# SSM outputs spilled in four parts and reloaded into slots of their own, softmax reciprocals spread by a TensorE product, and two buffers for the SSM input operator

## The chip, the core and the metric

The kernel runs on one core of a Trainium2 chip. A core has five engines that each work through an instruction list of their own, strictly in its order: PE (TensorE, matrix products), DVE (VectorE), ACT (ScalarE), POOL (GpSimd) and SP (SyncE, which here only issues DMAs). They wait for each other through semaphores. The metric is the device time of one execution in microseconds (us); less is better.

## What is computed

One layer of an encoder on 512 tokens of width 1024, cut here to its stages:

```
h = x + 1/2 * SwiGLU_1(RMSNorm(x))                      # FFN 1, width 2816
u = RMSNorm(h);  q, k, v, x_ssm, g_attn, g_ssm = split(u @ W_in)
y_attn = attention(rope(norm(q)), rope(norm(k)), v) @ W_attn_branch   # 8 heads of 64, 2 k/v heads
y_s5   = S5_forward(x_ssm) + S5_backward(x_ssm) + D * x_ssm           # 32 groups x 16 channels
z      = gelu(y_s5);  z = z * sigmoid(z @ W_glu + b_glu)
y_ssm  = z @ W_ssm_branch
h = h + (sigmoid(g_attn) * y_attn + sigmoid(g_ssm) * y_ssm) @ W_out
h = h + 1/2 * SwiGLU_2(RMSNorm(h))                      # FFN 2
out = h + sigmoid(RMSNorm(h) @ W_ple_gate) * (p @ W_ple_proj)
```

The softmax of a head is computed as exp(s - max), multiplied with v, and only then divided by the row sums. The reciprocals of these sums lie with one token per partition, and the products they scale have one channel per partition and the tokens along the free dimension, so the reciprocals have to be turned round and repeated over 64 partitions.

## The kernel before

Each float32 product is made of three products of a high and a low part (`mm3`, lines 559 to 561), with 512 columns of output in one PSUM bank. A weight chunk is loaded by SP (`wchunk`, L554), split into its two parts by ACT (L544) and DVE (L545), and then used by PE. There are four raw buffers and four of each part. Tile names in the trace end in letters such as `w_617h` for the high part of weight chunk 617.

The part that the change touches is the mixer, from 440 to 730 us of the trace:

1. **Projections.** x_ssm (tile `X`) goes to DRAM (`xs_d`) and comes back in another layout as `U`, which ACT and DVE split into three bf16 parts (L33 to L36). k, v (`pk`) and q (`pq`) follow.
2. **SSM blocks.** 16 blocks (`ssm_block`) of two groups each. In a block PE multiplies `U` with the input operator `wv` into `pv` (24 small products, L43). DVE then runs nine operations: a rotation (L463 to L465), two scans (L473, L474), the rotation back (L477 to L479). PE adds the direct part (`ml`, L43) and the output operator (`wol`, L485) into `py`, and ACT writes the gelu into tile `Z`. The operators of a block are prefetched by SP: `wv` has one buffer, the table `tbl`, `wol` and `ml` two each. Between the blocks stand products of the twelve first gates (`gate`, bank `pi`, 24 products each), and DVE also does q's rotary embedding and normalisation.
3. **Attention.** For each head `scores` makes four products pairs `sc`, DVE a negated maximum (`nb`), ACT the exponentials `p` with their sums (`s2`). `values` transposes `p` on PE (`ppt`, 4 x 128x128), ACT and DVE split the result into `ph` and `pl`, PE multiplies with v into `po`. At the end of a head ACT copies half of `po` to `ob` and DVE adds the other half into `of`. After each second head `of` is multiplied with `R`, the reciprocals spread over partitions, and split into `oT`. `fill` gives PE other work beside the heads: four more gates, then the GLU of z (`w_521`, `w_554` are its weight chunks), then the SSM branch.

After the last block `Z` goes to DRAM in 8 DMAs (`zs_d`). `z_load` brings it back with channels on partitions as four tiles `zT`, which ACT and DVE split into `z`. The four `zT` lie in slots of the normalised input (`x4l` to `x7l`), which the gates' products read. The reciprocals go to DRAM as `r_d`, one 4-byte number after the other, and come back as `R` by a DMA that repeats each row over 64 partitions. All of these DMAs are in SP's list, between the weight loads.

A scheduler sets the order of the instructions on each engine from the program, with priorities; a tile's slot is handed on when its last reader is done.

Of the kernel before, what the change touches and what calls it, by code (L numbers as in the profile page):

```python
# [17 lines left out]
P = 128  # L18
SEQ = 512
# [408 lines left out]
def ssm_prefetch(nc, sp, k, j):  # L428

    d = k["ops"]  # L430
    b, q = j * GM // GB, j * GM % GB
    wv = sp.tile([P, 3, GM, 2 * P], BF16, tag="wv", name=f"wv{j}")
    nc.sync.dma_start(wv, d["wv"][b].rearrange("p (i g m) -> p i g m", i=3, g=GB)[:, :, q:q + GM])
    tb = sp.tile([P, 6, GM * NC_], F32, tag="tbl", bufs=2, name=f"tbl{j}")
    src = d["tb"][b].rearrange("p (i n) -> p i n", i=5)
    nc.sync.dma_start(tb[:, :5], src[:, :, q * NC_:(q + GM) * NC_])
    nc.sync.dma_start(tb[:, 5], src[:, 4, q * NC_:(q + GM) * NC_])
    wo = sp.tile([P, GM, 2 * P], F32, tag="wo", bufs=2, name=f"wol{j}")
    nc.sync.dma_start(wo, d["wo"][b].rearrange("p (g m) -> p g m", g=GB)[:, q:q + GM])
    mm = sp.tile([P, 3, GM, P], BF16, tag="m", bufs=2, name=f"ml{j}")  # L440
    nc.sync.dma_start(mm, d["m"][:, :, j * GM:(j + 1) * GM])
    return wv, tb, wo, mm
# [65 lines left out]
def kernel(  # L508
# [21 lines left out]
    def uid(s):  # L530
        _u[0] += 1
        return f"{s}_{_u[0]}"
# [25 lines left out]
    def mm3(o, ah, al, bh, bl, start, stop):  # L558
        T.matmul(o, ah, bh, start=start, stop=False)  # L559
        T.matmul(o, ah, bl, start=False, stop=False)  # L560
        T.matmul(o, al, bh, start=False, stop=stop)  # L561


    def xg_tiles(tagp, n):
# [212 lines left out]
    def proj_tok(banks, c0, n, kn):  # L777

        for kc in range(KT // kn):
            wh, wl = wchunk(win[kc * kn * P:(kc + 1) * kn * P, c0:c0 + n], kn, n)  # L780
            for t in range(TT):
                for k in range(kn):
                    kk = kc * kn + k
                    tk = slice(t * P, (t + 1) * P)
                    mm3(banks[t][:, :n], xg[kk][0][:, tk], xg[kk][1][:, tk], wh[:, k], wl[:, k],
                        kk == 0, kk == KT - 1)

    def gate(m):
        dst = (ta + ts)[m]
# [4 lines left out]

        return proj_T(GA0 + m * P, done)

    ts = []
    ta = [cp.tile([P, SEQ], F32, tag=f"h{m}", name=f"ta{m}") for m in range(KT)]
    qT = [slot(mp, f"q{hd}", 1, "qT", F32R) for hd in range(NH)]
# [8 lines left out]
    with tc.tile_pool(name="qp", bufs=1, reuse_waits="tile") as qp:  # L808
# [51 lines left out]
            headsum(ks[t], 2, t, NH)  # L860
            rope(ks[t], ks[t], 2, 1, t)
        pq = [bank("mm", f"pq{t}") for t in range(TT)]
        proj_tok(pq, Q0, 512, 2)
        qs = [qp.tile([P, NH, HD], F32, name=f"qs{t}") for t in range(TT)]
        for t in range(TT):
            S.activation(qs[t].rearrange("p h d -> p (h d)"), pq[t], AF.Copy, scale=rt[:, t:t + 1])
# [38 lines left out]
    def scores(hd):  # L905

        g = hd // (NH // 2)
        pr = prs.setdefault(hd, [])
        nb = a0.tile([P, TT], F32, tag="nb", bufs=3, name=uid("nb"))
        if hd % 2 == 0:  # L910
            sums2[hd // 2] = a0.tile([P, 2, TT], F32, tag="s2", bufs=2, name=uid("s2"))
        sm = sums2[hd // 2][:, hd % 2]
        for t in range(TT):
            sc = bank("mm", uid("sc"))
            tk = slice(t * P, (t + 1) * P)
            T.matmul(sc, qT[hd][:, tk], kh[g], start=True, stop=False)
            T.matmul(sc, qT[hd][:, tk], kl[g], start=False, stop=True)  # L917
            V.tensor_reduce(nb[:, t:t + 1], sc, axis=AX.X, op=ALU.max, negate=True)  # L918
            p_ = slot(pool_p[hd % 2], "pp", 4, "p")
            S.activation(p_, sc, AF.Exp, bias=nb[:, t:t + 1], accum_out=sm[:, t:t + 1])  # L920
            pr.append(p_)
            yield
        if hd % 2 == 1:
            s2 = sums2[hd // 2]
            V.reciprocal(s2, s2)
            nc.sync.dma_start(r_d[hd // 2].rearrange("h (t p) -> p h t", p=P), s2)

    prs, sums2 = {}, {}
    r_d = [dp.tile([2, SEQ], F32, name=f"r_d{j}") for j in range(NH // 2)]
    Z = sp.tile([P, G, NC_], F32, tag="U", name="Z")  # L930
    for j in range(NM):
        with tc.high_priority():
            py = ssm_block(nc, sp, ps, pre, U3, j)
        if j < NM - 1:
            pre = ssm_prefetch(nc, sp, kd, j + 1)
        S.activation(Z[:, j * GM:(j + 1) * GM].rearrange("p g c -> p (g c)"), py[:, :GM * NC_], AF.Gelu_apprx_tanh)
        if j % 2 == 0 and j // 2 < NG2:
            run(gate(NG1 + j // 2))
        if j == NM - 2:
            run(scores(0))  # L940
    zv = zs_d.rearrange("(g c) (l n) -> l c g n", c=CH, l=L)
    for l in range(L):
        nc.sync.dma_start(zv[l], Z[l * CH:(l + 1) * CH])
    sx.close()

    at = mx.enter_context(tc.tile_pool(name="at", bufs=1, reuse_waits="tile"))
    pool_p[1] = at
    ph_ = lambda name, dt=F32: slot(at, "ph", 8, name, dt)


    ohl, po_of = [], {}
# [1 line left out]
    def values(hd):  # L953
        pr = prs[hd]
        g = hd // (NH // 2)
        po = bank("pv", uid("po"))
        for kt in range(TT):
            pt = bank("pt", uid("ppt"))
            for t in range(TT):
                T.transpose(pt[:, t * P:(t + 1) * P], pr[t][:, kt * P:(kt + 1) * P], ident)  # L960
            ph, pl = ph_("ph", F32R), ph_("pl", F32R)
            split(ph, pl, pt)
            yield
            vv = vhl[:, kt, g].rearrange("p a d -> p (a d)")
            T.matmul(po, vv, ph, start=kt == 0, stop=False)  # L965
            T.matmul(po, vv, pl, start=False, stop=kt == TT - 1)
        if hd % 2 == 0:
            po_of[hd // 2] = slot(at, "of", 3, "of")
        of = po_of[hd // 2]
        ob = at.tile([HD, SEQ], F32, tag="ob", bufs=1, name=uid("ob"))  # L970
        S.copy(ob, po[HD:])
        V.tensor_add(of[(hd % 2) * HD:(hd % 2 + 1) * HD], po[:HD], ob)
        if hd % 2 == 1:
            R = at.tile([P, SEQ], F32, tag="R", bufs=1, name=uid("R"))
            for i in range(2):
                nc.sync.dma_start(R[i * HD:(i + 1) * HD], r_d[hd // 2][i].partition_broadcast(HD))
            V.tensor_mul(of, of, R)
            ohl.append(tuple(slot(at, f"o{c}{hd // 2}", 1, "oT", F32R) for c in "hl"))
            split(ohl[hd // 2][0], ohl[hd // 2][1], of)
# [3 lines left out]

    def z_load():
        xs_ = lambda k, c, name, dt=F32: slot(xp, f"x{k}{c}", 1, name, dt)
        hb = at.tile([P, 4], F32, name="hb")
        nc.gpsimd.dma_start(hb, w["ssm_glu_b"][0].rearrange("(m p) -> p m", p=P))
        V.tensor_scalar_mul(hb, hb, 0.5)
        zs.append((hb, xs_))
        for m in range(4):  # L990
            zT = xs_(4 + m, "l", "zT")
            nc.sync.dma_start(zT, zs_d[m * P:(m + 1) * P])
            zh, zl = xs_(m, "h", "z", F32R), xs_(m, "l", "z", F32R)
            split(zh, zl, zT)
            zs.append((zT, zh, zl))
# [182 lines left out]
```

## Time and profile before

| | us |
|---|---|
| three runs | 1200.87, 1204.99, 1205.73 (median 1204.99) |
| the profiled execution | 1204.96 |
| its span, first to last instruction | 1203.1 |
| PE busy | 1145.5 (95%) |
| DVE busy | 762.0 (63%) |
| ACT busy | 487.2 (41%) |
| mean granted clock of PE | 0.987 of full speed |

How to read it: a row of the timeline gives the start, the duration and, in brackets, how long its engine sat idle before it and what ended the idle time. PE's rows overlap: a 128x512 product is listed with 0.39 us, and the next starts 0.23 us later. Where the clock column says 0.50 PE runs at half of its full clock. A row of windows gives each engine's busy time in a stretch, then the granted clock, the share of the 16 DMA engines that is busy, and GB/s.

### The profile page before, as it was taken

How to read it: one execution, taken by the hardware profiler on the slowest of the kernel's cores; microseconds unless marked ns; L12 is line 12 of the kernel's file. 1: busy time of each engine (PE TensorE's matmuls, PEld its weight loads, DVE VectorE, ACT ScalarE, POOL GpSimd, SP SyncE). 2: the span in 40 equal slices, each digit the busy share in tenths (PEclk: the TensorE clock that was granted, in tenths of full speed). 3: DMA queues.
4: the chain of work that ended last, by engine and by line, in shares of the span. 5: the costliest groups of instructions: out<-in, count | busy, mean ns of one | idle time of the engine just before them, and what ended most of it. 6: DMA issues, size and time to landing. Idle time of an engine off the chain costs nothing.

```text
span 1203.1 us, 15745 instructions
## 1 busy us (share of the span) xinstructions
PE 1145.5 (95%) x5836; PEld 942.7 (78%) x5836; DVE 762.0 (63%) x1502; ACT 487.2 (41%) x882; POOL 48.8 (4%) x81
## 2 busy tenths in 40 slices
PE   4999979999999998998996999999999999999998
PEld 3788758888788887887785778888888888888886
DVE  3896699965798656998565847654443344444543
ACT  4583454543444425523355734332322232323331
POOL 4123100000000000000000000000000000000100
PEclk9999989999999999999997999999999999999999
DMA  9549754546967948886622225433323433223422
GB/s 182 137 108 309 233 186 154 175 114 144 283 213 239 287 142 135 232 261 189 177 64 59 62 62 159 121 89 89 93 72 97 129 99 97 85 73 96 149 61 53
DMA packets 254397, 171.73 MB, mean 143 GB/s; under 512 B 38928, under 2 KB 233680, under 8 KB 254320
## 3 DMA queue, kind: packets, MB, share of 16 engines
q1 hardware_dynamic: 249936, 158.46, 46.5%
q0 software_dynamic: 3920, 11.15, 3.7%
q10 hardware_dynamic: 464, 1.11, 0.5%
q8 instruction: 46, 0.75, 0.3%
q14 instruction: 31, 0.25, 0.1%
HBM read 146.79 MB, written 35.49 MB: 152 GB/s over the span
## 4 chain that ended last, share of the span: by engine, by line
PE 72%; DVE 10%; DMA 9%; ACT 4%; SPq 3%; issue 3%; ACTq 0%; DVEq 0%
PE pd L560 7%; PE pd L561 6%; PE pd L559 6%; PE pg L559 6%; PE pg L560 6%; PE pg L561 6%; PE pu L561 5%; PE pu L559 5%; PE pu L560 5%; DMA d_tb<-tst 2%; DMA w<-in_ffn_w_up_dram 2%; PE pi L560 2%; PE pi L559 2%; PE pi L561 2%; SPq L403 1%
## 5 line engine op out<-in xcount | busy, mean ns | idle before, releaser
L686 DVE TENSOR_TENSOR t<-pu,rb 128x512 f32<-128x512 f32 x44 | 30.3, 690 | 79.7 <-PE pu L561 79.5
L684 DVE TENSOR_TENSOR t<-pg,rb 128x512 f32<-128x512 f32 x44 | 30.3, 689 | 52.1 <-PE pg L561 50.5
L544 ACT CAST ah<-t 128x512 fp32r<-128x512 f32 x44 | 27.4, 622 | 53.6 <-DVE t L687 53.4
L704 DVE SCALAR_TENSOR_TENSOR h<-pd,h 128x512 f32<-128x512 f32 x32 | 22.1, 690 | 33.1 <-PE pd L561 33.0
L685 ACT ACTIVATE t<-t 128x512 f32<-128x512 f32 x44 | 27.7, 632 | 22.0 <-DVE t L684 21.4
L545 DVE TENSOR_TENSOR al<-t,ah 128x512 fp32r<-128x512 f32 x44 | 30.2, 687 | 6.5 <-ACT ah L544 6.2
L687 DVE TENSOR_TENSOR t<-t,t 128x512 f32<-128x512 f32 x44 | 30.3, 690 | 2.5 <-ACT t L685 0.4
L918 DVE TENSOR_REDUCE nb<-sc 128x1 f32<-128x512 f32 x32 | 21.3, 684 | 10.2 <-PE sc L917 10.2
L569 ACT ACTIVATE xh<-h,gains 128x512 fp32r<-128x512 f32 x32 | 22.7, 722 | 11.0 <-DVE h L704 8.8
L1083 POOL DMA_DIRECT2D pin<-in_p_dram x8 | 4.2, 526 | 539.7 <-PE pd L560 534.5
L570 DVE SCALAR_TENSOR_TENSOR xl<-h,gains,xh 128x512 fp32r<-128x512 f32 x32 | 23.8, 744 | 0.8 <-ACT xh L569 0.3
L545 DVE TENSOR_TENSOR pl<-ppt,ph 128x512 fp32r<-128x512 f32 x32 | 21.6, 684 | 3.0 <-ACT ph L544 2.7
L544 ACT CAST ph<-ppt 128x512 fp32r<-128x512 f32 x32 | 18.5, 587 | 11.8 <-PE ppt L960 11.5
L920 ACT ACTIVATE p<-sc,nb 128x512 f32<-128x512 f32 x32 | 21.9, 693 | 2.8 <-PE ppt L960 1.7
L960 PE MATMUL ppt<-ident,p 128*128 128x128 f32 x128 | 21.3, 282 | 1.8 <-ACT p L920 1.8
L43 PE MATMUL pv<-U,wv 128*128 128x64 bf16 x384 | 14.5, 196 | 8.5 <-DMA wv<-d_wv 6.1
L43 PEld LDWEIGHTS <-wv 128*128 128x128 bf16 x384 | 12.9, 100 | 12.1 <-DMA wv<-d_wv 7.3
L965 PE MATMUL po<-ph,vhl 128*128 128x512 f32 x32 | 14.4, 452 | 8.2 <-ACT ph L544 8.1
L646 PE MATMUL xT<-ident,xt 128*128 128x128 f32 x32 | 7.8, 424 | 15.0 <-DMA xt<-in_x_dram 15.0
L960 PEld LDWEIGHTS ppt<-ident,p 128*128 128x128 f32 x128 | 16.9, 146 | 6.5 <-ACT p L920 2.2
L485 PE MATMUL py<-vv,wol 128*128 128x64 f32 x128 | 20.0, 279 | 0.8 <-DVE vv L478 0.7
L646 PEld LDWEIGHTS xT<-ident,xt 128*128 128x128 f32 x32 | 6.3, 224 | 16.1 <-issue 15.1
(1962 smaller groups left out, 3854.8 us busy)
## 6 DMA issues: line engine op xcount, KB each, us to landing
w<-in_ffn_w_gate_dram SPq DMA_DIRECT2D x44, 512.0 KB
w<-in_ffn_w_up_dram SPq DMA_DIRECT2D x44, 512.0 KB
w<-in_w_in_dram SPq DMA_DIRECT2D x26, 512.0 KB
w<-in_ffn_w_down_dram SPq DMA_DIRECT2D x32, 384.0 KB
w<-in_ffn_w_down_dram SPq DMA_DIRECT2D x32, 320.0 KB
d_wv<-wv SPq DMA_DIRECT2D x8, 768.0 KB
wv<-d_wv SPq DMA_DIRECT2D x16, 384.0 KB
d_tb<-tst SPq DMA_DIRECT2D x8, 640.0 KB
```

What stands on the lines that cost most here:

```text
L43: nc.tensor.matmul(o, a[i], b[j], start=start and n == 0, stop=stop and n == 5)
L544: S.copy(hi, src)
L545: V.tensor_sub(lo, src, hi.bitcast(F32))
L559: T.matmul(o, ah, bh, start=start, stop=False)
L560: T.matmul(o, ah, bl, start=False, stop=False)
L561: T.matmul(o, al, bh, start=False, stop=stop)
L570: V.scalar_tensor_tensor(x[1], src, gain, x[0].bitcast(F32), mul, sub))
L684: V.tensor_mul(t1, gu[0], rb)
L685: S.activation(t1, t1, AF.Silu)
L686: V.tensor_mul(t2, gu[1], rb)
L687: V.tensor_mul(t1, t1, t2)
L960: T.transpose(pt[:, t * P:(t + 1) * P], pr[t][:, kt * P:(kt + 1) * P], ident)
```

## The change

It has four parts.

- `wv` gets two buffers.
- `Z` is spilled after each fourth block, 8 DMAs of 16x8x64 each time (32 in all, with as many bytes as the 8 before), and the spills and the four loads of `zT` are issued by POOL. `zT` has four tiles of its own in the pool `at`; the slots for `ph` and `pl` go from eight to six, and `R`'s tile in SBUF is dropped. The GLU bias `hb` is loaded before the projections.
- `R` comes from PE: ACT repeats the reciprocals of two heads along the free dimension into a tile `rr`, in the one slot of `ob`, and PE multiplies each of its four 128x128 pieces with the identity into a PSUM bank of the kind `pt`, of which there are two (shared with `ppt`). `r_d` and its DMAs are gone.
- The first SSM block may not be issued before the last product of q's projection.

```diff
-    wv = sp.tile([P, 3, GM, 2 * P], BF16, tag="wv", name=f"wv{j}")
+    wv = sp.tile([P, 3, GM, 2 * P], BF16, tag="wv", bufs=2, name=f"wv{j}")
...
-        proj_tok(pq, Q0, 512, 2)
+        last_q = proj_tok(pq, Q0, 512, 2)
...
-            nc.sync.dma_start(r_d[hd // 2].rearrange("h (t p) -> p h t", p=P), s2)
...
+    zv = zs_d.rearrange("(g c) (l n) -> l c g n", c=CH, l=L)
     for j in range(NM):
-        with tc.high_priority():
+        with tc.high_priority(), (tc.issue_after(last_q.ins) if j == 0 else ExitStack()):
             py = ssm_block(nc, sp, ps, pre, U3, j)
...
+        if j % 4 == 3:
+            gs = slice((j - 3) * GM, (j + 1) * GM)
+            for l in range(L):
+                nc.gpsimd.dma_start(zv[l][:, gs], Z[l * CH:(l + 1) * CH, gs])
...
-    for l in range(L):
-        nc.sync.dma_start(zv[l], Z[l * CH:(l + 1) * CH])
...
-    ph_ = lambda name, dt=F32: slot(at, "ph", 8, name, dt)
+    ph_ = lambda name, dt=F32: slot(at, "ph", 6, name, dt)
+    zTs = [slot(at, f"zT{m}", 1, "zT") for m in range(4)]
+    for m in range(4):
+        nc.gpsimd.dma_start(zTs[m], zs_d[m * P:(m + 1) * P])
...
-        ob = at.tile([HD, SEQ], F32, tag="ob", bufs=1, name=uid("ob"))
+        ob = slot(at, "ob", 1, "ob")[:HD]
...
-            R = at.tile([P, SEQ], F32, tag="R", bufs=1, name=uid("R"))
-            for i in range(2):
-                nc.sync.dma_start(R[i * HD:(i + 1) * HD], r_d[hd // 2][i].partition_broadcast(HD))
+            rr = slot(at, "ob", 1, "rr").rearrange("p (t h d) -> p t h d", t=TT, h=2)
+            S.copy(rr, sums2[hd // 2].rearrange("p h t -> p t h").unsqueeze(3).broadcast_to([P, TT, 2, HD]))
+            rr = rr.rearrange("p t h d -> p t (h d)")
+            R = bank("pt", uid("R"))
+            for t in range(TT):
+                T.matmul(R[:, t * P:(t + 1) * P], rr[:, t], ident, start=True, stop=True)
...
-            zT = xs_(4 + m, "l", "zT")
-            nc.sync.dma_start(zT, zs_d[m * P:(m + 1) * P])
+            zT = zTs[m]
```

**Place 1, the start of the SSM blocks on PE.** Before, block 0's first products stand in the middle of q's projection; `w_330h` is the second of q's four weight chunks:

```order
L559 MATMUL pq3_4482<-w_330h_4514,xh_39_301 128x512
L560 MATMUL pq3_4482<-w_330l_4515,xh_39_301 128x512
L561 MATMUL pq3_4482<-w_330h_4514,xl_40_302 128x512
L559 MATMUL pq3_4482<-w_330h_4514,xh_41_303 128x512
L43 LDWEIGHTS wv0_4114
L43 MATMUL pv0_5037<-U32_4125,wv0_4114 128x64
```

Now they stand behind the last product of the fourth chunk, and blocks 0 and 1 alternate:

```order
L559 MATMUL pq3_4485<-w_332h_4577,xh_49_311 128x512
L560 MATMUL pq3_4485<-w_332l_4578,xh_49_311 128x512
L561 MATMUL pq3_4485<-w_332h_4577,xl_50_312 128x512
L43 LDWEIGHTS wv0_4117
L43 MATMUL pv0_5036<-U32_4128,wv0_4117 128x64
L43 LDWEIGHTS wv1_5093
L43 MATMUL pv1_5136<-U32_4128,wv1_5093 128x64
```

50 products of q's projection have moved ahead of the first block.

**Place 2, the first product with `rr`.** On DVE the rows between the gate's product and the scaling now are these (`po_425` is the second head's output, `ob_450` its copied half, `R_452` the new product):

```order
L793 TENSOR_TENSOR ts_376_5031<-pi_486_6652,rb_286_4081 128x512
L922 TENSOR_REDUCE nb_487_6659<-sc_499_6707 128x1
L545 TENSOR_TENSOR w_620l_7145<-w_620_7143,w_620h_7144 128x1024
L979 TENSOR_TENSOR of_423_6404<-po_425_6409,ob_450_6513 64x512
L922 TENSOR_REDUCE nb_487_6659<-sc_504_6732 128x1
L987 TENSOR_TENSOR of_423_6404<-of_423_6404,R_452_6518 128x512
```

and on PE, from the last product into `po_425` on:

```order
L973 MATMUL po_425_6409<-pl_447_6494,vhl_4113 128x512
L920 MATMUL sc_499_6707<-kh_296_4110,qT_291_4105 128x512
L921 MATMUL sc_499_6707<-kl_298_4112,qT_291_4105 128x512
L920 MATMUL sc_504_6732<-kh_296_4110,qT_291_4105 128x512
L921 MATMUL sc_504_6732<-kl_298_4112,qT_291_4105 128x512
L986 MATMUL R_452_6518<-ident_69,rr_451_6516 128x128 x4
L967 MATMUL ppt_456_6529<-ident_69,p_434_6438 128x128
```

Before, there was no product of this kind; four score products stand between the head's end and it.

**Place 3, the last product with `rr`.** Before, PE's rows from the last head's last product (`po_613`) on begin so, with nine products of the attention branch (`pg_656`) up to the first that reads the last `oT`:

```order
L966 MATMUL po_613_7105<-pl_628_7172,vhl_4110 128x512
L559 MATMUL pg_656_7341<-oT_448_6490,w_650h_7314 128x512
L560 MATMUL pg_656_7341<-oT_449_6491,w_650h_7314 128x512
L561 MATMUL pg_656_7341<-oT_448_6490,w_650l_7315 128x512
L559 MATMUL pg_656_7341<-oT_503_6714,w_650h_7314 128x512
L560 MATMUL pg_656_7341<-oT_504_6715,w_650h_7314 128x512
L561 MATMUL pg_656_7341<-oT_503_6714,w_650l_7315 128x512
L559 MATMUL pg_656_7341<-oT_584_6991,w_650h_7314 128x512
L560 MATMUL pg_656_7341<-oT_585_6992,w_650h_7314 128x512
L561 MATMUL pg_656_7341<-oT_584_6991,w_650l_7315 128x512
L559 MATMUL pg_640_7269<-oT_631_7191,w_639h_7264 128x512
```

Now these nine stand ahead of the head's end, and only the new product lies between it and the first reader:

```order
L967 MATMUL ppt_629_7194<-ident_69,p_613_7124 128x128
L973 MATMUL po_616_7133<-pl_627_7182,vhl_4113 128x512
L972 MATMUL po_616_7133<-ph_630_7199,vhl_4113 128x512
L973 MATMUL po_616_7133<-pl_631_7200,vhl_4113 128x512
L986 MATMUL R_634_7217<-ident_69,rr_633_7215 128x128 x4
L559 MATMUL pg_644_7301<-oT_635_7223,w_643h_7296 128x512
```

On ACT the copy into `rr_633` stands directly behind the copy into `ob_632`, and both use the same slot.

## Rows read from the trace of the kernel before

**Rows 1.** PE's waits from 440 to 760 us: total, times, longest.
```profile
PE po L965 <- ACT ph L544: 8.1, 1, 8.1
PE pv L43 <- DMA wv<-d_wv: 6.1, 4, 3.6
...
PE sc L916 <- DVE ts L792: 1.2, 1, 1.2
```

**Rows 2.** Timeline of ACT and PE at the longest wait.
```profile
640.59 0.62 ACT L544 CAST z<-zT 128x512 fp32r<-128x512 f32 x1 [12.69 <-DMA zT<-zs_d]
...
641.75 0.80 PE L965 MATMUL po<-ph,vhl 128*128 128x512 f32 x1 [8.10 <-ACT ph L544]
```

**Rows 3.** Windows there: length, busy PE, PEld, DVE, ACT, POOL, clock, DMA share, GB/s.
```profile
634.00:640.00 6.00, 0.00 (x0) 0.00 (x0) 0.00 (x0) 0.00 (x0) 0.00 (x0) 0.87 0.40 32
640.00:642.00 2.00, 0.25 (x1) 0.26 (x1) 0.76 (x2) 1.23 (x3) 0.00 (x0) 0.50 0.97 293
...
652.00:654.00 2.00, 2.00 (x10) 1.54 (x10) 0.61 (x2) 0.00 (x0) 0.00 (x0) 0.99 0.08 22
```

**Rows 4.** SP's queue: its timeline around the loads of zT, and its longest wait.
```profile
628.17 0.37 SPq L926 DMA_DIRECT2D r_d<-s  x1
628.63 5.13 SPq L992 DMA_DIRECT2D zT<-zs_d  x4
...
SPq L976 <- DMA r_d<-s: 29.2, 3, 10.0
```

**Rows 5.** The SSM stage: one window, and DVE's two main waits in it.
```profile
466.00:584.00 118.00, 108.55 (x1021) 92.00 (x1020) 106.90 (x246) 45.77 (x130) 0.00 (x0) 0.99 0.75 219
...
DVE tt L463 <- PE pv L43: 3.5, 2, 2.0
DVE tt L463 <- DMA tbl<-d_tb: 3.1, 2, 1.9
```

**Rows 6.** Timeline of DVE and PE: the stage's first and last operations.
```profile
466.31 1.29 DVE L34 TENSOR_TENSOR Ur<-U,U 128x512 f32<-128x512 f32 x2 [6.68 <-ACT U L33]
469.13 0.86 PE L43 MATMUL pv<-U,wv 128*128 128x64 bf16 x24 [2.38 <-DVE U L36]
...
583.42 0.28 DVE L479 TENSOR_TENSOR vv<-te 128x128 f32<-128x128 f32 x1
586.22 0.55 PE L485 MATMUL py<-vv,wol 128*128 128x64 f32 x4
...
592.10 0.39 PE L916 MATMUL sc<-kh,qT 128*128 128x512 f32 x1
```

**Rows 7.** A window behind PE's wait of 3.55 us (556.42).
```profile
558.00:560.00 2.00, 2.00 (x14) 1.39 (x12) 1.94 (x4) 0.59 (x1) 0.00 (x0) 0.53 0.25 68
```

**Rows 8.** Float32 products of 128x128 pieces: durations in ns, first and last start.
```profile
L368 PE MATMUL p<-cT,bb x8: 275/275/342, 253.8 to 255.3; 128*128 128x128 f32 x8
...
L370 PE MATMUL p<-cT,nbi x8: 275/275/275, 254.1 to 255.5; 128*128 128x128 f32 x8
```

**Rows 9.** Timeline of ACT, DVE and PE at the end of the last head.
```profile
715.64 0.58 ACT L971 COPY ob<-po 64x512 f32<-64x512 f32 x1 [5.73 <-PE po L966]
716.26 0.68 DVE L972 TENSOR_TENSOR of<-po,ob 64x512 f32<-64x512 f32 x1 [5.62 <-ACT ob L971]
716.98 0.69 DVE L977 TENSOR_TENSOR of<-of,R 128x512 f32<-128x512 f32 x1
717.71 0.62 ACT L544 CAST oT<-of 128x512 fp32r<-128x512 f32 x1 [1.48 <-DVE of L977]
718.38 0.73 PE L559 MATMUL pg<-oT,w_639h 128*128 128x512 f32 x2 [0.66 <-ACT oT L544]
```

**Rows 10.** POOL's DMAs at the start of the kernel: durations, then time to landing.
```profile
L250 POOL DMA_DIRECT2D d_a<-d_at x16: 632/632/672, 83.2 to 116.6; - x16
...
DMA to landing us min/median/max: 6.0/11.1/17.3
```

**Rows 11.** DVE's timeline at 647 us: the low part of a weight chunk.
```profile
646.88 1.22 DVE L545 TENSOR_TENSOR w_617l<-w,w_617h 128x1024 fp32r<-128x1024 f32 x1
```

More of the change, by code (lines that the diff above doesn't have):

```diff
@@ L560, in mm3 @@
         T.matmul(o, ah, bl, start=False, stop=False)
-        T.matmul(o, al, bh, start=False, stop=stop)
+        return T.matmul(o, al, bh, start=False, stop=stop)
     def xg_tiles(tagp, n):
@@ L784, in proj_tok @@
                     tk = slice(t * P, (t + 1) * P)
-                    mm3(banks[t][:, :n], xg[kk][0][:, tk], xg[kk][1][:, tk], wh[:, k], wl[:, k],
-                        kk == 0, kk == KT - 1)
+                    last = mm3(banks[t][:, :n], xg[kk][0][:, tk], xg[kk][1][:, tk], wh[:, k], wl[:, k],
+                               kk == 0, kk == KT - 1)
+        return last
     def gate(m):
@@ L795, in gate @@
         return proj_T(GA0 + m * P, done)
+    hb = mp.tile([P, 4], F32, name="hb")
+    nc.gpsimd.dma_start(hb, w["ssm_glu_b"][0].rearrange("(m p) -> p m", p=P))
+    V.tensor_scalar_mul(hb, hb, 0.5)
     ts = []
@@ L925, in scores @@
             V.reciprocal(s2, s2)
-            nc.sync.dma_start(r_d[hd // 2].rearrange("h (t p) -> p h t", p=P), s2)
     prs, sums2 = {}, {}
-    r_d = [dp.tile([2, SEQ], F32, name=f"r_d{j}") for j in range(NH // 2)]
     Z = sp.tile([P, G, NC_], F32, tag="U", name="Z")
+    zv = zs_d.rearrange("(g c) (l n) -> l c g n", c=CH, l=L)
     for j in range(NM):
-        with tc.high_priority():
+        with tc.high_priority(), (tc.issue_after(last_q.ins) if j == 0 else ExitStack()):
             py = ssm_block(nc, sp, ps, pre, U3, j)
@@ L940 @@
             run(scores(0))
-    zv = zs_d.rearrange("(g c) (l n) -> l c g n", c=CH, l=L)
-    for l in range(L):
-        nc.sync.dma_start(zv[l], Z[l * CH:(l + 1) * CH])
     sx.close()
@@ L985, in z_load @@
         xs_ = lambda k, c, name, dt=F32: slot(xp, f"x{k}{c}", 1, name, dt)
-        hb = at.tile([P, 4], F32, name="hb")
-        nc.gpsimd.dma_start(hb, w["ssm_glu_b"][0].rearrange("(m p) -> p m", p=P))
-        V.tensor_scalar_mul(hb, hb, 0.5)
         zs.append((hb, xs_))
         for m in range(4):
-            zT = xs_(4 + m, "l", "zT")
-            nc.sync.dma_start(zT, zs_d[m * P:(m + 1) * P])
+            zT = zTs[m]
             zh, zl = xs_(m, "h", "z", F32R), xs_(m, "l", "z", F32R)
```

## Prediction

> **What bounds the kernel now.** The share of busy time on the page comes first: PE is busy for 95% of the span, so what can be won is PE's idle time and the time at half of its clock, and what can be lost is anything that lets PE stand still or gives it more to do. PE's waits in the mixer come second [rows 1]: one wait of 8.1 us, a product of the last head that waits for ACT's `ph`. The timeline there [rows 2] shows why ACT is late: the cast of `zT`, which stands ahead of `ph` in ACT's list, waited 12.69 us for its DMA. The windows [rows 3] show the DMA engines 40% busy from 634 to 640 us and yet moving 32 GB/s; from 640 to 642 us they move 293. SP's queue [rows 4] says what ran first: `r_d`, numbers of 4 bytes one after the other, issued at 628.17, some 10 us for each such DMA to be done; `zT` was issued behind it at 628.63. So the wait has two causes, the late issue (`zT` takes the slots of tiles that the gates read) and the slow `r_d` ahead of it.
>
> The clock is third. It is 0.87 over 634 to 640 us, which is 1.56 us at half of full speed, hence from 638.4; at 652 it is back [rows 3]. Half clock is 1.2 GHz, full 2.4.
>
> Last the SSM stage [rows 5]: over 466 to 584 us DVE is busy for 106.9 of 118 us, and its main waits are 3.5 us for `pv` and 3.1 for `tbl`. There DVE sets the pace. PE fills its time with gates; the scores after the stage start at 592.10, 8.4 us after DVE's last operation ends at 583.70 [rows 6].
>
> **The change, part by part.** Durations come from the profiled execution, 1204.96 us with a span of 1203.1; the median of the runs shown is 1204.99, so both may be read as one.
>
> *zT in slots of its own, loaded by POOL: −13.7.* Nothing of `r_d` is left, and the loads wait only for the last spills. The last block's gelu should be done near 578 us (below); 8 spills at 0.63 us to issue and four loads at the same price [rows 10] are 7.6 us, and two landings, each at the longest of those rows, 17.3, make 35: 620 at the latest, against some 628 when ACT had come to the cast before. The wait of 8.1 and the one of 1.2 for `sc`, which stands just behind it, go [rows 1]. The clock goes too: from 641.75 to 652.0 are 10.25 us, less the 1.2, so about 8.9 at half clock, of which 4.4 are given back. If a part of the wait only moves, it is this term that shrinks.
>
> The Trainium skill speaks against POOL here ("DMA: Bandwidth & Descriptors", section "SWDGE vs HWDGE vs iDMA"): DMAs that GpSimd issues have their descriptors built by software, while those of SP come from hardware, with a faster setup. POOL's own rows of this kernel show 0.63 us for an issue and 6.0 to 17.3 us to the landing [rows 10]; by either, the loads have time to spare.
>
> *32 spills in place of 8, off SP's list: 0.* The bytes are the same; POOL does nothing else there, its busy time is 0.00 [rows 5].
>
> *The SSM stage with two `wv`, begun later: −2.0 (−5.5 to +5).* PE's waits for `wv`, 6.1 us in four [rows 1], vanish, but DVE leads there, so they count only as far as DVE had to wait for `pv`. DVE's first operation of the stage starts at 466.31; to 583.70 are 117.4 us, and 110.8 without the two waits. By the order, two low-part splits (1.22 each, [rows 11]) and one gate product (0.69, as a row of that shape in [rows 9]) move behind the stage's last operation: 107.7. I start it 0.5 later (`hb`'s small product and the longer queue), and leave 1.5 us of idle out of a possible 0 to 7, since the second `wv` should let `pv` run ahead while `tbl` has its two buffers as before. It ends at 466.8 + 107.7 + 1.5 = 576.0. Block 0 itself is later, behind 50 products of q, but DVE has q's rotary embedding to do meanwhile. Behind DVE's last operation PE has the last `py`, two rows of 0.55 [rows 6], and by the order 57 gate products that used to lie earlier, 13.0 us at 0.23: the scores start at 590.1 instead of 592.10.
>
> *R by TensorE, its work: +3.8.* Four products are made of four 128x128 pieces each. The nearest rows are float32 pieces of that shape [rows 8]: 16 records, alternating between two lines of the code, the first of one at 253.8 and the last of the other at 255.5, so 15 steps in 1.7 us, 0.115 each. The two lines run four times each, which makes eight products: a float32 product has two records, 0.23 us, and four of them 0.92, with the end of the last 0.95. Should these pieces need one record each, it is half of that, and at worst each takes the 0.275 of its row alone: 0.45 to 1.1. I take 0.95, since rows of the same shape and type give it. Times four, 3.8 (1.8 to 4.4).
>
> *R by TensorE, its waits: +7.85.* The four places differ in what PE has to do between a head's end and the product.
> The first, `R_452` (place 2): `rr` takes the slot of `ob`, so it waits for DVE's addition that reads `ob`. DVE's list ahead of that is a gate product, a maximum, a weight split of 1.22 [rows 11] and the addition, 0.68, each other about 0.7 [rows 9]; then ACT's copy, 0.62 as a cast of 128x512. From the last `po` on that is 3.6 to 3.9. PE has four score products, 0.9, and stands for 2.6 (0 to 3). Its bank of the kind `pt` then goes back to `ppt` only after DVE's scaling: 1.05 more. Together 3.65.
> The second, `R_508`: 12 products cover `rr`, and the bank costs 0.45. The third, `R_586`, has 32 products and costs nothing.
> The last, `R_634` (place 3): before, the chain was copy 0.58, addition 0.68, scaling 0.69, cast 0.62, and nine products of the attention branch ran beside it; 0.66 stayed open [rows 9]. Now those nine stand ahead of the head's end. The chain is `ob`, addition, `rr`, four pieces, scaling, cast: 0.58 + 0.68 + 0.62 + 0.95 + 0.69 + 0.62 = 4.1, with the hand-overs 4.4 from the last `po`, of which the pieces' 0.95 is work already counted: 3.5 idle. That the last `ppt` is followed by no product any more, until `ph` and `pl` are there, adds 0.9. 4.4 − 0.66 = 3.75.
>
> *The clock behind these waits: +2.55.* After a wait of 2.38 us [rows 6] no drop shows up in the windows; after one of 3.55 us, at 556.42, the clock is 0.53 [rows 7], and 3.4 us at half speed cost 1.7. The last place is as long as the second, so 1.7; the first, 2.6, lies between, so half of it, 0.85 (0 and 1.7).
>
> Fewer slots for `ph` and `pl` cost nothing as long as no more than two sets stand ahead of their `po`, and by the order none do. What would cover for them otherwise is the fillers.
>
> The sum: −13.7 − 2.0 + 3.8 + 3.65 + 0.45 + 3.75 + 2.55 = −1.5, that is 1203.5. With the ends of the terms its own range is 1197 to 1209.
>
> **The rivals.**
> *The products with R find cover (1193).* If DVE does the addition earlier than I think, or the clock holds, the waits of the first and the last place and their clock go: 3.65 + 3.75 + 2.55 = 10, and 1193.5 stays. For it: DVE is less than half busy in the attention. Against: at the last place nothing stands beside the chain in any engine's order.
>
> *DVE starves in the SSM stage (1213, slower).* Pairs of blocks now alternate on PE, with gate products between them, and block k+2's `pv` stands behind 5 to 7 us of these; `tbl` and `wv` share SP's list with the weights, which wait for raw buffers, and the DMA engines are 75% busy there [rows 5] before the spills. If each of eight pairs costs DVE 1.4 us, the idle time is 11 instead of 1.5, and the time 1213. It decides for slower from an idle time of 9 us on; before, the two waits are 6.6 with one `wv`, which speaks against it.
> The Trainium skill ("Trainium Kernel Development and Optimization", section "Key Constraints") has the queues of SP and POOL share the same DMA engines, so that moving spills to POOL saves only issue time; no run here shows it yet for these spills.
>
> *The loads by POOL come too late (1217).* Then the wait for `zT` stays and the R terms are paid in full: 1203.5 + 13.7. It needs `z` to land past 628, which is 50 us after the last gelu, three times the longest landing [rows 10].
>
> **How the numbers follow.** My forecast has 0.50, the covered R 0.26, the starved DVE 0.14, the late loads 0.04; 0.06 is left to what I don't see. Half a per cent, 6 us, is about what a measurement of this kernel can tell from no change. Faster: the covered R and a little of my own case's lower end, 0.31. Slower: 0.14 + 0.04 + a part of the rest, 0.19. The same: 0.50. The range runs from the covered R, 1192.5, to the starved DVE, 1213.
>
> **What would show it.** In the changed kernel's profile ACT's cast of `zT` should have no wait and POOL's loads should land before 620. DVE's last operation of the SSM blocks should end near 576 and the first `sc` start near 590; DVE's waits for `pv` and `tbl` there should sum to 1.5, and if to over 9, I am wrong on the slow side. PE's waits for `rr` should be about 2.6 at the first product, none at the third, 3.5 for `oT` and `rr` together at the last, each of the long ones with a stretch at half clock behind it. R's four pieces should take 0.95 us; at 0.45, 2.0 of my sum are gone.

## The result, and the profile after

The changed kernel takes 1212.65 us (median of five runs, 1208.17 to 1213.27) against 1203.27 for the one before in the same session; the ratio is 1.0065, with a 95% interval of 1.0037 to 1.0093. It is slower, by about 8 us. 1203.5 had been forecast.

The profiled execution shows less of it, 1208.71 with a span of 1206.9. It came to q's projection earlier: the first product of q starts at 452.01 us, before at 456.14. The kernel b_R below, which changes nothing ahead of that product, has 451.91; why was not looked into. From there to the end it took 754.9 us, before 747.0, which is 7.9 more. All the parts below are counted from this product on.

PE's waits in the mixer of the changed kernel (us in total, times, longest):

```profile
PE R L986 <- ACT rr L982: 4.5, 2, 2.5
PE py L43 <- DMA ml<-d_m: 2.5, 4, 1.1
PE kt L899 <- DVE qT L890: 2.1, 1, 2.1
...
PE py L485 <- DMA wol<-d_wo: 1.5, 3, 0.6
PE pg L559 <- ACT oT L544: 1.4, 1, 1.4
```

The wait of 8.1 us for `ph` [rows 1] is gone, and so are the waits for `wv`. In their place stand waits for the product with `rr`, short ones for the two other operators of the SSM blocks, and one of 2.1 us for DVE's `qT`. ACT's timeline shows the casts of `zT` without a wait, where it had been 12.69 us [rows 2]:

```profile
626.20 1.15 ACT L544 CAST z<-zT 128x512 fp32r<-128x512 f32 x2
627.90 1.16 ACT L544 CAST z<-zT 128x512 fp32r<-128x512 f32 x2
```

POOL's loads of `zT` (duration of an issue in ns, first and last start, then the time to landing) were there at 590, long before:

```profile
L955 POOL DMA_DIRECT2D zT<-zs_d x4: 536/546/569, 583.1 to 585.2; - x4
...
DMA to landing us min/median/max: 4.1/4.2/4.4
```

The end of the last head, which answers to [rows 9], on ACT, DVE and PE:

```profile
714.29 0.58 ACT L978 COPY ob<-po 64x512 f32<-64x512 f32 x1 [1.31 <-PE po L973]
714.90 0.68 DVE L979 TENSOR_TENSOR of<-po,ob 64x512 f32<-64x512 f32 x1 [1.21 <-ACT ob L978]
715.62 0.62 ACT L982 COPY rr<-s 128x512 f32<-128x512 f32 x1 [0.75 <-DVE of L979]
716.29 1.16 PE L986 MATMUL R<-ident,rr 128*128 128x128 f32 x8 [2.04 <-ACT rr L982]
717.49 0.69 DVE L987 TENSOR_TENSOR of<-of,R 128x512 f32<-128x512 f32 x1 [1.90 <-PE R L986]
718.21 0.62 ACT L544 CAST oT<-of 128x512 fp32r<-128x512 f32 x1 [1.97 <-DVE of L987]
718.88 1.22 PE L559 MATMUL pg<-oT,w_643h 128*128 128x512 f32 x2 [1.43 <-ACT oT L544]
```

Each step waits for the one above it, and PE sits idle for 2.04 and 1.43 us around its one product, where it had been 0.66.

What the waits don't show is the clock. Windows of the changed kernel in the SSM stage and behind the two products with `rr` (busy time of PE, PEld, DVE, ACT, POOL, then the granted clock, DMA share, GB/s):

```profile
500.00:504.00 4.00, 3.12 (x52) 2.89 (x49) 3.92 (x14) 0.63 (x1) 0.00 (x0) 0.89 0.69 200
504.00:506.00 2.00, 2.00 (x12) 1.81 (x10) 1.95 (x5) 0.56 (x2) 0.24 (x1) 0.50 1.04 322
530.00:534.00 4.00, 2.18 (x50) 1.88 (x47) 2.45 (x5) 0.00 (x0) 0.00 (x0) 0.98 0.87 238
534.00:540.00 6.00, 6.00 (x25) 5.13 (x23) 5.66 (x16) 0.55 (x2) 3.73 (x8) 0.50 1.00 300
558.00:562.00 4.00, 0.94 (x15) 0.46 (x13) 3.89 (x7) 2.33 (x4) 1.70 (x4) 0.89 0.70 229
562.00:566.00 4.00, 3.16 (x10) 2.67 (x11) 3.81 (x11) 0.59 (x1) 0.00 (x0) 0.50 0.33 99
...
632.00:636.00 4.00, 1.55 (x9) 1.11 (x10) 3.10 (x4) 1.75 (x4) 0.00 (x0) 1.00 0.25 78
636.00:640.00 4.00, 4.00 (x18) 3.05 (x17) 2.58 (x4) 1.68 (x3) 0.00 (x0) 0.57 0.15 53
712.00:718.00 6.00, 2.74 (x15) 1.61 (x13) 1.89 (x3) 1.78 (x3) 0.00 (x0) 1.00 0.00 0
718.00:724.00 6.00, 5.12 (x12) 4.11 (x13) 2.99 (x6) 2.29 (x4) 0.00 (x0) 0.51 0.00 0
```

Read them in pairs: a stretch in which PE has gaps, and then one at half clock. In the SSM stage this happens three times, with no wait above 2.14 us beside it (that one, for `qT`, ends at 562.84); before it happened once there, behind a wait of 3.55 us [rows 7].

**PE's losses.** For every kernel below, two losses of PE were added up in its trace: its waits, and what the clock took (in windows of 2 us, one minus the granted clock, times PE's busy time). "Stage" is from the first product of q to the first score product, "behind" from there to 300 us after that first product of q. "Between" counts the q and gate products that PE's order puts between the first product of the first SSM block and the last of the last. Each row of losses comes from one execution; the changed kernel and a_rdma, whose order of products in the stage is the same, differ there by 0.7 us. Labels with b_ start from the kernel before, the others from the changed one; the experiments say what each is.

| | ratio, 95% interval | between | stage: idle, clock | behind: idle, clock |
|---|---|---|---|---|
| before | 1 | 317 | 9.3, 1.6 | 12.1, 4.4 |
| changed | 1.0065 (1.0037 to 1.0093) | 231 | 7.7, 7.7 | 10.9, 4.7 |
| b_z | 0.9900 (0.9875 to 0.9924) | 331 | 8.8, 4.7 | 2.8, 0.0 |
| b_zslots | 0.9897 (0.9881 to 0.9913) | 330 | 9.4, 4.4 | 2.8, 0.0 |
| b_R | 1.0055 (1.0032 to 1.0078) | 317 | 8.8, 4.5 | 12.8, 4.3 |
| b_wv2 | 1.0126 (1.0104 to 1.0147) | 213 | 17.0, 9.8 | 13.6, 4.1 |
| a_wv1 | 1.0001 (0.9988 to 1.0014) | 312 | 5.3, 2.9 | 12.0, 4.3 |
| a_spillend | 1.0060 (1.0038 to 1.0082) | 225 | 7.5, 8.1 | 10.8, 5.8 |
| a_noafter | 1.0145 (1.0121 to 1.0169) | 218 | 16.4, 8.9 | 11.6, 4.2 |
| a_ml3only | 1.0044 (1.0029 to 1.0060) | 219 | 8.7, 6.3 | 11.7, 4.0 |
| c_wv1_rr | 0.9953 (0.9938 to 0.9969) | 312 | 4.3, 1.7 | 9.6, 2.9 |
| a_rdma | 0.9922 (0.9910 to 0.9935) | 231 | 10.9, 5.2 | 2.8, 0.0 |
| d_late1 | 0.9884 (0.9869 to 0.9898) | 312 | 4.5, 1.7 | 4.6, 2.9 |
| a_spaced | 1.0074 (1.0058 to 1.0089) | 266 | 10.9, 2.5 | 11.9, 3.9 |
| a_rdma_all3 | 0.9936 (0.9914 to 0.9959) | 216 | 9.1, 6.8 | 2.8, 0.0 |
| a_all3 | 1.0087 (1.0060 to 1.0114) | 216 | 8.7, 8.0 | 11.5, 5.5 |
| g_even2 | 0.9866 (0.9845 to 0.9886) | 288 | 5.8, 3.4 | 3.4, 1.7 |
| a_even | 1.0027 (1.0009 to 1.0045) | 288 | 6.0, 6.3 | 11.0, 4.3 |

The four sums give the change: waits 18.6 against 21.4, clock 12.4 against 6.0, and 3.9 of work for the four products with R: −2.8 + 6.4 + 3.9 = 7.5, of the 7.9 that the trace shows.

### The profile page after: what moved, and what is told of

Read it like the earlier page. It is cut to its first block, busy times and chain, and to the rows that moved or that the text cites. A ratio compares the mean times of both kernels' runs of the same rounds, so it can differ in the third digit from the quotient of the medians.

```text
span 1206.9 us, 15820 instructions
## 1 busy us (share of the span) xinstructions
PE 1155.9 (96%) x5868; PEld 951.0 (79%) x5868; DVE 760.8 (63%) x1502; ACT 490.3 (41%) x886; POOL 67.5 (6%) x117
## 4 chain that ended last, share of the span: by engine, by line
PE 76%; DVE 8%; DMA 8%; ACT 3%; issue 2%; SPq 2%; ACTq 0%; DVEq 0%
PE pd L560 6%; PE pd L561 6%; PE pd L559 6%; PE pg L559 6%; PE pg L560 6%; PE pg L561 6%; PE pu L561 5%; PE pu L559 5%; PE pu L560 5%; DMA d_tb<-tst 3%; PE pi L559 2%; PE pi L560 2%; PE pi L561 2%; DMA w<-in_ffn_w_up_dram 2%; SPq L403 1%
## 5 line engine op out<-in xcount | busy, mean ns | idle before, releaser
L544 ACT CAST ph<-ppt 128x512 fp32r<-128x512 f32 x32 | 18.5, 589 | 17.2 <-PE ppt L967 16.9
L943 POOL DMA_DIRECT2D zs_d<-Z x32 | 16.7, 531 | 150.2 <-ACT Z L939 150.2
L485 PEld LDWEIGHTS py<-vv,wol 128*128 128x128 f32 x128 | 18.1, 204 | 2.8 <-DVE w_383l L545 0.8
L939 ACT ACTIVATE Z<-py 128x128 f32<-128x128 f32 x16 | 4.3, 278 | 33.1 <-PE py L485 32.8
```

Source lines behind the costliest of these rows:

```text
L485: nc.tensor.matmul(o, wo[:, g, ri * P:(ri + 1) * P], E[:, ri, g * NC_:(g + 1) * NC_], start=False, stop=ri == 1)
L544: S.copy(hi, src)
```

## The experiments

**The wait for z.** Three kernels start from the one before. The z part alone (spills, loads by POOL and slots as in the change, `R` by DMA as before; `ph` and `pl` get five slots for the room):

```diff
-            zT = xs_(4 + m, "l", "zT")
-            nc.sync.dma_start(zT, zs_d[m * P:(m + 1) * P])
+            zT = zTs[m]        # loaded by POOL behind the spills
```

> The kernel before with the z part alone: spills after each fourth block and loads of zT by POOL into slots of their own, ph and pl with five slots, one operator buffer, reciprocals by DMA as before. By the prediction's term this is worth 13.7 us: 0.987 to 0.991, with no wait of ACT for zT. Theory O (any edit makes the scheduler lay out the SSM stage anew, and that moves the time by several us either way): the wait for zT is gone as well, but the SSM stage's idle and half clock differ from before by 3 us or more.

Ratio 0.990. Behind the stage 2.8 us of idle and no half clock are left of 12.1 and 4.4: 13.7 us, the term of the prediction. The stage lost 2.6 more than before (13.5 against 10.9), close to the 3 that theory O had asked for: an edit elsewhere moved it. Then the slots alone, with 8 spills and the loads in SP's list:

```diff
-                nc.gpsimd.dma_start(zv[l][:, gs], Z[l * CH:(l + 1) * CH, gs])
+        nc.sync.dma_start(zv[l], Z[l * CH:(l + 1) * CH])   # once, behind the last block
...
-        nc.gpsimd.dma_start(zTs[m], zs_d[m * P:(m + 1) * P])
+        nc.sync.dma_start(zTs[m], zs_d[m * P:(m + 1) * P])
```

> The kernel before with slots of their own for zT and nothing moved to POOL: 8 spills and the four loads by SP after the last block, ahead of r_d in SP's list. PE's order is that of the z part alone but for one product. If the slots are the cause of the wait, it is gone as with the z part alone: 0.988 to 0.992. If POOL's list and the early spills were needed, zT is late by several us again: 0.996 to 1.000.

0.9897: the same. SP issued the loads at 601.40 and `r_d` only at 607.25, so z was ahead of it. POOL and the early spills bring nothing; the slots do it. And the product for the reciprocals alone, z as before:

```diff
-            nc.sync.dma_start(r_d[hd // 2].rearrange("h (t p) -> p h t", p=P), s2)
...
+            for t in range(TT):
+                T.matmul(R[:, t * P:(t + 1) * P], rr[:, t], ident, start=True, stop=True)
```

> The kernel before with the product for the reciprocals alone: no DMAs of r_d, zT still in the slots that the gates read and loaded by SP. The product's work (4.0 us), its waits (7) and their clock (4 to 5) are paid; the wait for zT shrinks, since no 4-byte DMA stands ahead of it any more, by 4 to 8 us with its clock. Sum: 1.004 to 1.010. If the wait for zT stays at 8 us, it was the slots alone that made it late, and the time is 1.012 or more.

1.0055, in the range. SP's queue and ACT's timeline of this kernel:

```profile
625.91 3.76 SPq L993 DMA_DIRECT2D zT<-zs_d  x4
```

```profile
628.51 1.38 ACT L544 CAST z<-zT 128x512 fp32r<-128x512 f32 x2 [3.13 <-DMA zT<-zs_d]
```

The loads are as late as before (628.63 in [rows 4]), in the slots of the gates, and yet ACT waits 3.13 us instead of 12.69, and PE not at all. So of the two causes either one alone had to go: early slots, or no 4-byte DMA ahead. The change removes both, and the second is paid for in full.

**The second operator buffer.** Four kernels test what makes the stage lose more; theories W, S and L are those of the expectations. First one buffer again:

```diff
-    wv = sp.tile([P, 3, GM, 2 * P], BF16, tag="wv", bufs=2, name=f"wv{j}")
+    wv = sp.tile([P, 3, GM, 2 * P], BF16, tag="wv", name=f"wv{j}")
```

> The changed kernel with one buffer for the SSM operator again. In the changed kernel PE stands at half clock for about 17 us between q's projection and the first scores, against 3.4 us before. Theory W: the second buffer lets two blocks stand side by side on PE, small products and short waits in one stretch, and these pull the clock down; then half clock there falls to 5 us or less and the time to 1.001 to 1.003 of before. Theory S (the spills in the middle of the stage crowd the block loads) and theory L (the late start packs 16 blocks into less time than their loads take): nothing changes there, 1.005 to 1.008.

1.0001, and 8.2 us of loss in the stage instead of 15.4; the intervals lie apart. Half clock in the stage is 6.8 us where theory W had 5 or less, and the time lies just below the range it gave: W holds here in its direction. The reverse, the buffer put alone into the kernel before:

> The kernel before with the second buffer for the SSM operator and nothing else. Theory W: two stretches or more at half clock appear in the SSM stage, 1.003 to 1.006. Theories S and L: waits for the operator (6.1 us) go and nothing else comes, 0.997 to 1.000.

1.0126, more than any theory said. PE's waits in the stage:

```profile
PE pv L43 <- DMA wv<-d_wv: 5.5, 3, 3.5
PE kt L895 <- DVE qT L886: 3.8, 1, 3.8
PE py L485 <- DVE vv L478: 3.6, 2, 3.0
PE pv L43 <- DVE U L36: 3.2, 1, 3.2
```

A second buffer for `wv` leaves waits for `wv` of 5.5 us, nearly the 6.1 of before [rows 1], and adds waits for DVE. Without the late first block:

```diff
-        with tc.high_priority(), (tc.issue_after(last_q.ins) if j == 0 else ExitStack()):
+        with tc.high_priority():
```

> The changed kernel without the rule that the first block waits for the last product of q. Theory L: the blocks start some 8 us earlier and spread over 110 us and more, the waits for ml and wol go below 1.5 us, half clock there to 5 us or less, 1.000 to 1.003. Theories W and S: 1.005 to 1.008.

1.0145: theory L has the sign wrong, and theories W and S, for which nothing should change, miss it too. The late start helps, by 9.9 us in the stage. With the spills only at the end (`if j == NM - 1`, 8 DMAs by POOL):

> The changed kernel with all of Z spilled in 8 DMAs after the last block, by POOL, and zT still in slots of its own. Theory S: the waits for ml and wol (4.0 us) and the half clock behind them shrink by more than half, 1.000 to 1.003. Theories W and L: the SSM stage stays as it is, 1.005 to 1.008; z then lands some 5 us later and is still in time.

1.0060, the stage unchanged: theory S falls.

**What in the buffer costs.** First the short waits for `ml`, with a third buffer:

```diff
-    mm = sp.tile([P, 3, GM, P], BF16, tag="m", bufs=2, name=f"ml{j}")
+    mm = sp.tile([P, 3, GM, P], BF16, tag="m", bufs=3, name=f"ml{j}")
```

> The changed kernel with three buffers for ml, the operator whose short waits (2.5 us in four) stand ahead of the falls of the clock in the SSM stage. Theory M (these short waits are what pulls the clock down): half clock in the stage goes from 17 us to 10 or less, 1.001 to 1.004. Theory W in its plain form (two blocks side by side leave PE too little between them, whichever wait ends last): other waits take their place, 1.005 to 1.009.

1.0044, between the two: `ml`'s waits are 2.4 us as before, and others grew. Inconclusive, so the two operators got three buffers each, with the reciprocals by DMA and with the product (`bufs=3` for `ml` and `wol`, one for `vs`):

> The changed kernel with the reciprocals by DMA as before and with three buffers for ml and for wol, so that the second buffer of wv no longer makes these two the ones that come last (a buffer of vs is given up for the room). With two buffers the SSM stage had 10.9 us of idle, 9.4 of it waits for ml and wol, and 5.2 lost to the clock, ratio 0.992. Theory V (wv's second buffer moves the wait to the operators that still have two, and what was gained is lost there): the waits for ml and wol go below 3 us and the time comes to 0.984 to 0.988. Theory D (the blocks' loads as a whole do not come faster, and the next of them is late instead, or PE stands at half clock all the same): 0.990 to 0.994.

> The changed kernel with three buffers for ml and for wol, all else as changed, the product for the reciprocals included. In the changed kernel the SSM stage had 7.7 us of idle, 4.0 of it waits for ml and wol, and lost 7.7 to the clock. Theory V: most of that goes, 0.997 to 1.002 of before. Theory D: other waits take their place and the time stays at 1.004 to 1.008.

0.9936 and 1.0087, against 0.9922 and 1.0065 with two. The waits for `ml` and `wol` went below 3 us as theory V said, and nothing was gained by it: theory V falls. PE's waits in the stage of the first:

```profile
PE py L485 <- DVE vv L478: 4.7, 2, 3.0
...
PE py L485 <- DMA wol<-d_wo: 1.0, 1, 1.0
PE py L43 <- DMA ml<-d_m: 0.9, 1, 0.9
```

The waits for the loads have become waits for DVE. Then an order that keeps a block from beginning before the one two ahead of it has ended:

```diff
+            py, end = ssm_block(nc, sp, ps, pre, U3, j)
+        ends.append(end)       # ends starts as [last_q, None]; block j is issued after ends[j]
```

> The changed kernel, two operator buffers, with one more rule of order: a block may not begin on PE before the block two ahead of it has ended, so that after blocks 0 and 1 hardly two input products stand side by side. Theory W, with the order as what matters: the half clock in the SSM stage falls from 17 us to under 10 and the time to 1.000 to 1.003. Theory B (it is the loads of the second buffer that crowd the other operators' loads, whatever the order): ml and wol are still waited for, 1.004 to 1.008.

1.0074. The half clock went as theory W had it (2.5 instead of 7.7), but PE's idle time rose by 3.2 to 10.9, of which 7.6 are waits for `ml`. So this order neither speaks for W nor settles B.

**The product with R.** The changed kernel with `r_d` and its DMAs put back, all else kept:

> The changed kernel with the reciprocals by DMA as before (r_d and its two DMAs for each pair, ph and pl with five slots), all else as changed; PE's order in the SSM stage is the same as in the changed kernel. By the terms of the prediction the product costs 3.8 of work, 7.85 of waits and 2.55 of clock, in the changed kernel's profile 4.0, 7.1 and 4.7: 0.992 to 0.996 of before, that is 13 to 16 us less than the changed kernel. Rival: r_d delays z again, and part of it is lost: 0.998 to 1.002.

0.9922, which by the two ratios is 17.2 us less than the changed kernel (0.0143 times 1203), somewhat more than the 13 to 16 expected. PE's order in the stage is the same in both, so this is the price of the product. Behind the stage it is 3.9 of work, 8.1 of idle and 4.7 of clock: 16.7. With one buffer:

> The z part and the late first block together, one operator buffer, reciprocals by DMA as before, ph and pl with five slots. With one buffer and the late start the SSM stage had 5.3 us of idle and 2.9 lost to the clock, against 9.1 and 4.7 where the z part stood alone. Theory W (one buffer spaces the blocks, whatever else is done): these 5.6 us come on top of the z part's gain, 0.984 to 0.987 of before. Rival: the late start was paid for elsewhere (the last blocks run into the attention), and the time is that of the z part, 0.988 to 0.992.

0.9884. The stage loses 6.2, less than the 8.2 that theory W built on, but behind it 7.5 are lost instead of 2.8: the last blocks run into the attention, as the rival said (the first score starts at 578.82, the last product of the blocks at 591.90). So one buffer is worth 0.0038, 4.6 us, here. Then the product with cover: `rr` in a slot of its own, one buffer:

```diff
-            rr = slot(at, "ob", 1, "rr").rearrange("p (t h d) -> p t h d", t=TT, h=2)
+            rr = slot(at, "rr", 1, "rr").rearrange("p (t h d) -> p t h d", t=TT, h=2)
```

> The changed kernel with one buffer for the SSM operator and with rr in a slot of its own (ph and pl have five slots for it), so that rr no longer waits for the addition that reads ob and the product with it can be issued while the head's last products still run. Theory R (the waits at the first and the last product with rr cost 7 us and the half clock behind them 4 to 5): both go, 0.988 to 0.993 of before. Rival: the four products hold a bank that the transposes need, and the wait only moves there; 0.997 to 1.001, as with one buffer alone.

0.9953, about half of what was expected: 5.8 us better than a_wv1 and 8.3 worse than d_late1. PE's wait at the last head is now

```profile
PE pg L559 <- ACT oT L544: 2.8, 1, 2.8
```

so the wait for the product went into the wait for `oT` there, which had been 1.4 with `rr` in `ob`'s slot.

**The order.** In these runs the loss in the stage goes roughly with "between": 312 products, 6 to 8 us; 213 to 231, 15 to 27. But the four kernels with one buffer and the early start have 317 to 331 and lose 11 to 14, so the count alone does not set it. The last two kernels change the order alone, two buffers kept:

```diff
+            gs_.append(mm3(pg, wh[:, k], wl[:, k], xg[k][0], xg[k][1], k == 0, k == KT - 1))
...
+        with tc.high_priority(), tc.issue_after((gs_[n0 + 6 * j - 1] if j else last_q).ins):
```

> The kernel of a_rdma (two operator buffers, z part, late start, reciprocals by DMA) with one more rule of order: block j of the SSM stage may not begin on PE before 6j triples of gate products are done, so that 18 of them stand between any two blocks and none is left behind the last. In a_rdma 57 gate products stood behind the stage while PE was idle for 10.9 us in it and lost 5.2 to the clock. Theory F (with two buffers the order packs the blocks and holds products back that PE then lacks): idle and clock loss in the stage fall to 9 together, 0.982 to 0.988. Theory D (the loads or DVE set a pace at which PE loses the same, wherever the gates stand): 0.990 to 0.994.

> The changed kernel whole, with the same rule of order: 18 gate products between any two blocks. Theory F: the SSM stage's idle and clock loss, 15.4 us together, fall by 6 or more, 0.998 to 1.002 of before, what is then left of the loss being the product with rr. Theory D: 1.004 to 1.008.

Without the product 0.9866 against 0.9922 of a_rdma, the intervals apart: the loss in the stage falls from 16.1 to 9.2, the 9 that theory F gave; 2.3 of these 6.9 us come back behind the stage. Of PE's waits in the mixer of a_rdma

```profile
PE py L43 <- DMA ml<-d_m: 6.0, 4, 3.6
PE py L485 <- DMA wol<-d_wo: 3.4, 4, 1.8
```

g_even2 keeps, up to 600 us,

```profile
PE kt L902 <- DVE qT L893: 2.7, 1, 2.7
PE py L43 <- DMA ml<-d_m: 1.7, 2, 1.1
...
PE py L485 <- DMA wol<-d_wo: 0.2, 1, 0.2
```

A window of 140 us from q's projection on, PE alone, of a_rdma:

```profile
454.00:594.00 140.00, 128.92 (x1110) 0.95 0.76 209
```

and of g_even2:

```profile
454.00:594.00 140.00, 133.54 (x1140) 0.98 0.74 204
```

Busy time times clock is what PE got done in these 140 us: 122.5 and 130.9. The DMA engines moved no more in the second. The rule puts products between the blocks and by that also gives each block's loads more time; the two are not told apart by it. Three buffers for `ml` and `wol` shortened the waits for these loads without the order, and gained nothing.

With the product in, a_even comes to 1.0027, between the two theories; the interval overlaps that of the changed kernel. The stage of its profiled execution lost 12.3 instead of 15.4, half of the fall that theory F asked for. There the order is shown as a part of the cause at most.

## Why the prediction was wrong

It had the time at 1203.5, no change, and gave slower 0.19. By its steps:

- **zT, −13.7: right.** 13.7 in b_z, behind the stage. (In the working 10.25 less 1.2 is 9.05, not 8.9; it moves the term by less than 0.1.) That POOL would do no harm was right; that it was of use was not: b_zslots does without. The order that the Trainium skill gives ("DMA: Bandwidth & Descriptors", section "SWDGE vs HWDGE vs iDMA"), by which POOL's DMAs have the slower setup, agrees with the trace: an issue of these four loads took 0.55 us on POOL (b_z) and 0.43 on SP (b_zslots). In the time nothing of it shows, since either way the loads were there before ACT's cast.
- **The SSM stage, −2.0: the step that failed.** Measured +4.5 of loss (15.4 against 10.9), and +5.2 without the product. DVE did nearly what the step said: its waits for `tbl` and `pv` are 3.1 us instead of 6.6, and its last operation ends 121.6 us after q's first product, before 127.6, by the forecast 119.9. What failed is "DVE leads there", by which PE's own waits were to count only as far as DVE had to wait for them. DVE's waits in the changed kernel, and windows from q's first product to DVE's last operation and from there to the first score, of the changed kernel and then of the one before:

```profile
DVE tt L463 <- DMA tbl<-d_tb: 2.7, 2, 1.5
...
DVE tt L463 <- PE pv L43: 0.4, 1, 0.4
```

```profile
452.01:573.60 121.59, 113.93 (x1022) 97.17 (x1020) 105.67 (x251) 46.68 (x136) 12.56 (x24) 0.93 0.77 214
573.60:591.20 17.60, 17.60 (x99) 14.64 (x95) 4.97 (x6) 4.02 (x7) 6.34 (x12) 1.00 0.63 182
```

```profile
456.14:583.71 127.57, 118.11 (x1064) 99.91 (x1063) 109.66 (x255) 48.55 (x140) 0.00 (x0) 0.99 0.80 211
583.71:592.10 8.39, 8.39 (x52) 6.96 (x51) 1.85 (x2) 1.95 (x3) 0.00 (x0) 1.00 0.45 123
```

DVE is done 6.0 us earlier, and that is worth nothing, because behind it PE is busy without a gap for 17.6 us where it was 8.4: the scores wait for PE's list and not for DVE. The step had 14.1 there; the 57 gate products take the 13.0 that it gave them, but 3.5 us of products that stand ahead of them, before the last `py` is done, were left out. The whole stage takes 139.2 us, before 136.0, by the forecast 134.0. PE's work in it is about the same (123.8 and 125.1 us, without the losses), so what counts is what PE loses: 15.4 us of gaps and half clock instead of 10.9. Fewer products stand between the blocks as cover, 231 instead of 317. (Of the 86, 50 are q's, and moving those ahead helps by itself, as a_noafter shows; 36 are gate products that moved behind the last block. The step says that all 57 behind it used to lie earlier; 21 of them lay there before, too.) That the second buffer brings this loss is shown by a_wv1; that the order of the products makes it is shown without the product with R (g_even2), and with it only in part (a_even). Why a second buffer leads the scheduler to this order was not looked into.
- **The late first block** was costed at 0.5 us. It is worth 9.9 in the stage with two buffers (a_noafter) and 7.3 with one (b_z to d_late1), of which 4.7 are lost again behind it in the second case.
- **R, work +3.8: right.** The four products take 1.00 us (from 635.14 to the next `ppt` at 636.14), 0.89, 0.89 and 1.16: 3.9, with two records for each piece as the step had it.
- **R, waits +7.85: right in its sum, partly by luck.** 8.1 (10.9 behind the stage, 2.8 in a_rdma). Place 2 has 2.45 where 2.6 was forecast, and nothing of the 1.05 for its bank; the second product has 0.34 where 0.45 was; place 3 has 2.04 + 1.43 and two short ones ahead (0.45 and 0.22), 3.5 more than before, where 3.75 was. The other 1.9 are short waits for `p` and `pl` between 641 and 667 us that no term named.
- **R, clock +2.55: mis-sized.** 4.7. Behind the wait of 2.45 us the clock fell (the even chance came out against the kernel), and behind the last head it stayed at half for 6.8 us, twice what [rows 7] had given.

So of the 9 us by which the forecast missed, 6.5 lie in the stage and 2.2 in the clock behind R. Neither slow rival was it: DVE did not starve, z was not late. The covered R (1193) was tried, with one buffer, and brings 5.8, not 10.

## What to carry to other kernels

When an engine is busy for 95% of the time, an edit is judged by what this engine loses, its gaps and its clock. Work moved from inside a stage to behind it isn't neutral, even where another engine leads in the stage: it was the cover there. (Here this is shown in full only without the product with R.) And when a wait has two causes of which either one suffices, removing the cheaper one is enough: slots and loads moved within SP's list gave 1.0%, and the product that took `r_d` away cost 1.4%.

The kernel with the lowest median here, g_even2, keeps the slots for zT, the late start and both buffers, leaves the reciprocals to the DMA, and spaces the blocks by 18 gate products: 0.9866 of before, 1187.55 us. Its interval overlaps that of d_late1, which does without the second buffer and the spacing.

## What the runs showed of the hardware

The clock fell behind stretches in which no single wait was long: in the changed kernel the 4 us from 500 held waits of 0.47 and 0.41 us among small products, PE was busy for 3.12 of them, and half clock followed. It fell behind single waits too, one of 3.55 us before [rows 7] and one of 2.45 at the first product with `rr`; one of 1.73 us at 594.93 in the changed kernel passed without a fall. A list of the longest waits doesn't show the falls of the first kind; the windows with their clock do.

One DMA of 4 KB in 4-byte pieces held up the loads behind it in SP's list: with it `zT`, issued at 628.63, reached ACT's cast at 640.59; without it (b_R), issued at 625.91, at 628.51.
